# A hybrid mLSTM block: mLSTM of x in two chunks with a second state, and two scalings of the output by ScalarE

## The chip, the cores and the metric

The kernel runs on one core of a Trainium2 chip. The core has five engines that run side by side, each taking its own instructions in order: TensorE (PE in the profile; its weight loads are PEld), VectorE (DVE), ScalarE (ACT), GpSimd (POOL) and SyncE (SP), which here issues most DMAs. The metric is the device time of one execution in microseconds; lower is better. Three executions of the kernel before took 1530.03 to 1533.87 us, median 1532.19 us.

## The reference

Two layers work on x (512 tokens of 1024) and a context (256 tokens). Each layer has a token mixer (an mLSTM of 4 heads of 128, a Fourier mix and a convolution), whose outputs are joined and projected, and an MLP of width 4096. The last layer needs no output of the context. In the mLSTM a matrix state is carried over the tokens, forward and backward; the context is passed through first, and x starts from the context's last state. The reference does it in chunks of 64:

```python
def step(carry, inp):
    C, n, m = carry
    ...
    m_t = jnp.maximum(a, jnp.max(D, axis=-1))
    w_inter = jnp.exp(a - m_t)
    S = jnp.einsum('bhld,bhsd->bhls', qc, kc) * jnp.exp(D - m_t[..., None])
    num = w_inter[..., None] * jnp.einsum('bhed,bhld->bhle', C, qc) + jnp.einsum('bhls,bhse->bhle', S, vc)
    den = w_inter * jnp.einsum('bhd,bhld->bhl', n, qc) + jnp.sum(S, axis=-1)
    h = num / jnp.maximum(jnp.abs(den), jnp.exp(-m_t))[..., None]
    ...
    C_new = decay[..., None, None] * C + jnp.einsum('bhs,bhse,bhsd->bhed', ws, vc, kc)
    n_new = decay[..., None] * n + jnp.einsum('bhs,bhsd->bhd', ws, kc)
```

Forward and backward results are added, and each head's row of 128 is normalized: mean subtracted, multiplied by one over the deviation.

## The kernel before

Tokens stand as 6 blocks of 128: blocks 0 and 1 are the context, 2 to 5 are x. Matrix products with weights are done in three matmuls of a short and a rest part: a weight chunk comes by DMA into a tile `raw`, ScalarE rounds it to `hi` (line 219) and VectorE takes the rest as `lo` (line 220), for two weights ahead of their use. There are 3 tiles `raw`, 6 `hi` and 5 `lo`.

The mixer goes through the chunks of the input projection, for each head q, k and o (`stationary`, line 463). When a head's o is done, its `mlstm` is put on a list, and one of its three parts is written behind the matmuls of each of the next chunks: so the heads run between the projections of the next head. The three parts are these.

- First part: q and k are split into two parts each (`split`, lines 230 and 233). Scores are `scores` (line 793), three matmuls. For the context (layer 0 only) two key blocks against 256 queries; for x, four key blocks against all 512 queries. ScalarE makes the exponential weights from the stabilizers (line 836), GpSimd masks the block on the diagonal (line 771), VectorE multiplies by the scores (line 838). The context's state is made from k, transposed (line 818) and weighted by ScalarE (line 822), times v (line 842), copied to the tile `cs` (line 844). `qs` is q weighted for the state.
- Second part: for each block and direction TensorE sums the state term `qs` times `cs` and one term for each key block that the direction sees (line 862). All these are fp32 and 129 columns wide; column 128 is the denominator. Then `head_out`: VectorE makes the denominators, scales the forward part by the one (line 752), adds the backward part scaled by the other (line 753), and takes the moments. When all blocks of a group are there, GpSimd takes the power for the deviation (line 767), and VectorE subtracts the mean and scales (line 867).
- Third part: TensorE transposes the group's blocks (line 777), and ScalarE and VectorE apply gain and gate.

PSUM has 4 banks `mm` for projections and 4 `aux` for everything else. The order of the instructions on each engine is made by a scheduler, which places each when it expects its inputs to be ready, by a priority that follows the order in which the program is written. SyncE issues the loads; the stabilizers at a sequence's end are loaded to `m0` (line 647).

Of the kernel before, what the change touches and what calls it, by code (L numbers as in the profile page):

```python
# [50 lines left out]
XQ = CTX + 1  # L51
PAD = 15
# [12 lines left out]
def build(tc, a):  # L65
# [408 lines left out]
    def layer(l, res, nbg, first=None):  # L474
# [169 lines left out]

        m0 = small.tile([128, 2, 4], F32, tag="m0", name=nm("m0"))
        for d, t0 in ((0, CTX - 1), (1, 0)):
            dma(m0[:, d, :], md[l][4 * d:4 * d + 4, t0].partition_broadcast(128))

        def gate_columns():
            for q in range(2):  # L650
                ps = aux()
                for i in range(3):
                    T.transpose(ps[:, 128 * i:128 * i + 128], pm[:, 128 * (3 * q + i):128 * (3 * q + i) + 128], ident)
                v4 = ps[:, :384].rearrange("p (b g d n) -> p b g d n", b=3, g=2, d=2)
                for i in range(3):
                    V.tensor_copy(pcol[:, 3 * q + i], v4[:, i, 0, :, 0:4])
                    S.activation(em[:, 3 * q + i], v4[:, i, 1, :, 0:4], AF.Exp, scale=-1.0)
            for j in range(CB):
                V.tensor_tensor(wc[:, j], pcol[:, j], m0, ALU.subtract)
            S.activation(wc, wc, AF.Exp)  # L660

# [80 lines left out]
        def kcol(j):  # L742
            return 128 * j if j < CB else XQ + 128 * (j - CB)

        def head_out(ps, b, h, hn, ba):
            den = ps[:, 128:258:129]
            d = ty(2, "d")
            V.tensor_tensor(d, den, em[:, b, :, h], ALU.max)
            V.scalar_tensor_tensor(d, den, -1.0, d, ALU.mult, ALU.max)
            rd = ty(2, "rd")  # L750
            V.reciprocal(rd, d)
            V.tensor_scalar(hn, ps[:, 0:128], rd[:, 0:1], None, ALU.mult)
            V.scalar_tensor_tensor(hn, ps[:, 129:257], rd[:, 1:2], hn, ALU.mult, ALU.add)
            moments(hn, ba)
# [28 lines left out]
        def mlstm(h, q, k, to):  # L783
# [10 lines left out]

            if not last:
                mb = c2().rearrange("p (d t) -> p d t", d=2)
                dma(mb, mdv[h, :, 0:CTX].partition_broadcast(128))
                qk = aux()
                E = t4().rearrange("p (j d t) -> p j d t", j=2, d=2)
                for j in range(2):  # L800
                    scores(qk[:, 256 * j:256 * j + 256], 128 * j, 0, CTX)
                for j, d in ((0, 0), (0, 1), (1, 0), (1, 1)):
                    lo, hi = (128 * j, CTX) if d == 0 else (0, 128 * j + 128)
                    S.activation(E[:, j, d, lo:hi], mb[:, d, lo:hi], AF.Exp, scale=-1.0,
                                 bias=pcol[:, j, d, h:h + 1])
                    masked(E[:, j, d, 128 * j:128 * j + 128], d == 0)
                    V.tensor_tensor(E[:, j, d, lo:hi], E[:, j, d, lo:hi], qk[:, 256 * j + lo:256 * j + hi], ALU.mult)

                def c_terms(b, d, E=E):
                    js = range(0, b + 1) if d == 0 else range(b, CB)  # L810
                    return [(E[:, j, d, 128 * b:128 * b + 128], vt[h][:, j, :]) for j in js]
                groups.append((0, range(CB), c_terms))
            mb = t4().rearrange("p (d t) -> p d t", d=2)
            dma(mb, mdv[h, :, CTX:TOK].partition_broadcast(128))

            kp = aux()
            for j in range(CB):
                T.transpose(kp[:, 128 * j:128 * j + 128], k[:, 128 * j:128 * j + 128], ident)
            kw = c2().rearrange("p (d j n) -> p d j n", d=2, j=CB)
            for d in range(2):  # L820
                for j in range(CB):
                    S.activation(kw[:, d, j, :], kp[:, 128 * j:128 * j + 128], AF.Copy, scale=wc[:, j, d, h:h + 1])
            qs = t4().rearrange("p (d t) -> p d t", d=2)
            for d in range(2):
                S.activation(qs[:, d, :], mb[:, d, :], AF.Exp, scale=-1.0, bias=m0[:, d, h:h + 1])
            V.tensor_tensor(qs, qs, q[:, XQ:XQ + SEQ].unsqueeze(1).to_broadcast([128, 2, SEQ]), ALU.mult)
            Es = {}
            for j in range(CB, NB):
                qk = aux()
                scores(qk, kcol(j), XQ, SEQ)  # L830
                E = t4().rearrange("p (d t) -> p d t", d=2)
                Es[j] = E
                s0 = 128 * (j - CB)
                for d in range(2):
                    lo, hi = (s0, SEQ) if d == 0 else (0, s0 + 128)
                    S.activation(E[:, d, lo:hi], mb[:, d, lo:hi], AF.Exp, scale=-1.0, bias=pcol[:, j, d, h:h + 1])
                    masked(E[:, d, s0:s0 + 128], d == 0)
                    V.tensor_tensor(E[:, d, lo:hi], E[:, d, lo:hi], qk[:, lo:hi], ALU.mult)
# [15 lines left out]
            for t0, bs, terms in groups:  # L854
# [600 lines left out]
```

## Time and profile before

| | |
|---|---|
| median of 3 runs | 1532.19 us |
| the profiled execution | 1534.91 us, span 1532.9 us |
| TensorE busy | 1488.5 us, 97% |
| VectorE busy | 1101.4 us, 72% |
| ScalarE busy | 754.9 us, 49% |
| GpSimd busy | 94.0 us, 6% |
| granted TensorE clock | 0.998 |

The profile is of one execution; a time in it is counted from the start of the span. A group's row gives line, engine, operation, what it writes and reads, the shapes, how often (x), the busy time in us, the mean duration of one in ns, and the idle time of the engine before it with what ended it. Matmuls overlap, so a row's mean duration is more than what one takes from its neighbours. Lines are those of the kernel before unless the text speaks of the changed one.

### The profile page before, as it was taken

To read this page: it belongs to the slowest core of one execution; us is meant where nothing else is said; L and a number is where in the kernel's file an instruction comes from. 1 tells how busy PE (TensorE), PEld (TensorE's weight loads), DVE (VectorE), ACT (ScalarE), POOL (GpSimd) and SP (SyncE) were. 2 spreads that over 40 slices of the span, in tenths; PEclk is the share of its full clock that TensorE was granted. 3 is DMA by queue.
4 is the path that set the end of the run, shared out by engine and by line. 5 is a ranking of instruction groups with operands and counts; after the bars stand their busy time and mean duration, and the time that the engine had idled before them with its cause. 6 is when DMAs were issued, how large, how long until landed. Compare 5 with 4: busy or idle time off the path is not lost. (4 is left out here: it accounts for less than half of the span.)

```text
span 1532.9 us, 23301 instructions
## 1 busy us (share of the span) xinstructions
PE 1488.5 (97%) x8926; PEld 1303.6 (85%) x8926; DVE 1101.4 (72%) x2129; ACT 754.9 (49%) x1471; POOL 94.0 (6%) x233
## 2 busy tenths in 40 slices
PE   7999999999999999999999999999999999999998
PEld 4878888887888898898988979877888889999887
DVE  3359997754899886666865575898756886677666
ACT  4634245535745352442534576544437665555544
POOL 0002012200100000000000010111101000000000
PEclk9999999999999999999999999999999999999999
DMA  8445435523532452442622343422224133332224
GB/s 330 140 159 186 158 125 194 199 83 117 186 124 92 146 189 76 158 132 88 193 86 80 99 171 105 129 78 78 88 71 166 66 111 110 111 109 91 83 94 148
DMA packets 66015, 197.30 MB, mean 129 GB/s; under 512 B 11952, under 2 KB 14416, under 8 KB 65904
## 3 DMA queue, kind: packets, MB, share of 16 engines
q1 hardware_dynamic: 64464, 191.10, 37.5%
q0 software_dynamic: 1440, 4.72, 1.0%
q8 instruction: 70, 1.15, 0.3%
q14 instruction: 41, 0.34, 0.1%
HBM read 183.13 MB, written 12.66 MB: 128 GB/s over the span
## 5 line engine op out<-in xcount | busy, mean ns | idle before, releaser
L219 ACT ACTIVATE hi<-raw 128x1024 fp32r<-128x1024 f32 (+1 forms) x245 | 244.1, 999 | 397.0 <-PE mm L1052 134.9
L1052 PE MATMUL mm<-hi,t 128*128 128x512 f32 (+1 forms) x1296 | 406.1, 391 | 0.0
L220 DVE TENSOR_TENSOR lo<-raw,hi 128x1024 fp32r<-128x1024 f32 (+1 forms) x245 | 280.7, 1148 | 75.4 <-ACT hi L219 37.6
L1052 PEld LDWEIGHTS mm<-hi,t 128*128 128x128 f32 x1296 | 242.4, 188 | 54.7 <-DVE t L1220 0.4
L1052 PE MATMUL mm<-lo,t 128*128 128x512 f32 (+1 forms) x648 | 253.7, 391 | 0.0
L463 PE MATMUL mm<-hhi,hi 128*128 128x256 f32 (+1 forms) x576 | 168.3, 336 | 0.0
L463 PE MATMUL mm<-hlo,hi 128*128 128x256 f32 (+1 forms) x576 | 166.0, 332 | 0.0
L463 PE MATMUL mm<-hhi,lo 128*128 128x256 f32 (+1 forms) x576 | 165.0, 331 | 0.0
L1052 PEld LDWEIGHTS mm<-lo,t 128*128 128x128 f32 x648 | 121.8, 188 | 26.0
L1121 PE MATMUL mm<-hhi,hi 128*128 128x384 f32 (+1 forms) x448 | 139.5, 311 | 3.0 <-ACT c L1147 1.8
L1121 PE MATMUL mm<-hhi,lo 128*128 128x384 f32 (+1 forms) x448 | 138.5, 309 | 1.5 <-DVE lo L220 1.5
L1220 DVE TENSOR_TENSOR t<-mm,t 128x512 f32<-128x512 f32 x120 | 81.8, 688 | 79.5 <-PE mm L1052 79.4
L1121 PE MATMUL mm<-hlo,hi 128*128 128x384 f32 (+1 forms) x448 | 138.4, 309 | 0.0
L463 PEld LDWEIGHTS mm<-hhi,hi 128*128 128x128 f32 x576 | 107.1, 188 | 15.0 <-issue 2.5
L463 PEld LDWEIGHTS mm<-hhi,lo 128*128 128x128 f32 x576 | 108.3, 188 | 11.0
L463 PEld LDWEIGHTS mm<-hlo,hi 128*128 128x128 f32 x576 | 108.0, 188 | 11.0 <-issue 0.4
L679 DVE SCALAR_TENSOR_TENSOR t<-t,half,t 128x783 f32<-128x783 f32 (+1 forms) x120 | 102.3, 889 | 0.4
L1121 PE MATMUL mm<-t,hi 128*128 128x384 f32 (+1 forms) x448 | 97.4, 308 | 0.0
L1121 PEld LDWEIGHTS mm<-hhi,hi 128*128 128x128 f32 x448 | 84.4, 188 | 6.8 <-ACT c L1147 3.0
L1121 PEld LDWEIGHTS mm<-hhi,lo 128*128 128x128 f32 x448 | 84.3, 188 | 1.9 <-DVE lo L220 1.9
L1121 PEld LDWEIGHTS mm<-hlo,hi 128*128 128x128 f32 x448 | 84.4, 188 | 1.2
L233 DVE TENSOR_TENSOR t<-c,t 128x256 fp32r<-128x256 f32 (+1 forms) x132 | 62.2, 478 | 31.9 <-ACT t L230 31.5
(245 smaller groups left out, 2732.2 us busy)
## 6 DMA issues: line engine op xcount, KB each, us to landing
raw<-w SPq DMA_DIRECT2D x128, 512.0 KB, 4.3
raw<-w_at SPq DMA_DIRECT2D x48, 512.0 KB, 3.6
raw<-w_a SPq DMA_DIRECT2D x44, 512.0 KB, 4.3
raw<-w_c SPq DMA_DIRECT2D x32, 512.0 KB, 3.5
xd<-t SPq DMA_DIRECT2D x20, 512.0 KB, 2.9
raw<-w_o SPq DMA_DIRECT2D x16, 512.0 KB, 6.0
t<-xd SPq DMA_DIRECT2D x20, 256.0 KB, 6.0
t<-x SPq DMA_DIRECT2D x8, 512.0 KB, 6.0
```

The costliest lines, as they stand in the source:

```text
L219: S.activation(hi[:, r0:n0], raw[:, r0:n0], AF.Copy)
L220: V.tensor_tensor(lo[:, r0:n0], raw[:, r0:n0], hi[:, r0:n0].bitcast(F32), ALU.subtract)
L233: V.tensor_tensor(blk_lo, src, blk_hi.bitcast(F32), ALU.subtract)
L463: T.matmul(o[:, :n], wp[:, k, :], hp[:, k, t0:t0 + n], start=k == 0 and i == 0, stop=k == KB - 1 and i == 2)
L679: V.scalar_tensor_tensor(o, u[j][:, o0 + k:o1 + k], w, o, ALU.mult, ALU.add)
L1052: T.matmul(ps, hp[:, 128 * b:128 * b + 128], wp[:, f % 2, c0:c1], start=f == fs[0] and at[0] == 0 and n == 0, stop=f == fs[-1] and at[1] = ...
L1121: T.matmul(ps[:, :HN], wp[:, K2 * j + k, :], hp, start=first and k == 0 and i == 0, stop=k == K2 - 1 and i == 2, skip_group_check=True)
L1220: V.tensor_tensor(ac_, ps, ac_, ALU.add)
```

## The change

The 512 tokens of x are taken as two chunks of 256 (blocks 2, 3 and 4, 5). Scores are made within a chunk alone. What one chunk gives to the other comes through a state: forward the first chunk starts from the context's state `cs` and the second from a new state `cs1`, backward it is the other way round. `cs1` is the context's state times a decay, plus the weighted k of the chunk in between times v; for it four blocks of k are transposed and weighted as well, and two more columns of stabilizers are loaded to `m1`. The function `weighted` now serves the context and both chunks. Beside this, both scalings of a block's output are done by ScalarE; the second needs minus the mean times the scale, which VectorE makes in one small instruction a group.

```diff
+        m1 = small.tile([128, 2, 4], F32, tag="m1", name=nm("m1"))
+        dec = small.tile([128, 2, 4], F32, tag="dec", name=nm("dec"))
+        wx = small.tile([128, 4, 4], F32, tag="wx", name=nm("wx"))
+        for d, t0, t1 in ((0, CTX - 1, CTX + CH - 1), (1, 0, CTX + CH)):
             dma(m0[:, d, :], md[l][4 * d:4 * d + 4, t0].partition_broadcast(128))
+            dma(m1[:, d, :], md[l][4 * d:4 * d + 4, t1].partition_broadcast(128))
...
+            for i in range(4):
+                V.tensor_tensor(wx[:, i], pcol[:, CB + i, i // 2], m1[:, i // 2], ALU.subtract)
+            S.activation(wx, wx, AF.Exp)
+            V.tensor_tensor(dec, m0, m1, ALU.subtract)
+            S.activation(dec, dec, AF.Exp)
...
-            V.tensor_scalar(hn, ps[:, 0:128], rd[:, 0:1], None, ALU.mult)
+            S.activation(hn, ps[:, 0:128], AF.Copy, scale=rd[:, 0:1])
             V.scalar_tensor_tensor(hn, ps[:, 129:257], rd[:, 1:2], hn, ALU.mult, ALU.add)
...
+            def weighted(mb, kc, q0, blk):
+                qk = aux()
+                E = t4().rearrange("p (j d t) -> p j d t", j=2, d=2)
+                for j in range(2):
+                    scores(qk[:, CH * j:CH * j + CH], kc + 128 * j, q0, CH)
...
+            kp = aux()
+            for i in range(4):
+                T.transpose(kp[:, 128 * i:128 * i + 128], k[:, XQ + 128 * i:XQ + 128 * i + 128], ident)
+            for i in range(4):
+                S.activation(kx[:, i, :], kp[:, 128 * i:128 * i + 128], AF.Copy, scale=wx[:, i, h:h + 1])
...
-            for j in range(CB, NB):
-                qk = aux()
-                scores(qk, kcol(j), XQ, SEQ)
...
+            Ex = [weighted(mb[:, :, CH * c:CH * c + CH], XQ + CH * c, XQ + CH * c, CB + 2 * c) for c in range(2)]
...
+            cp = aux()
+            for d in range(2):
+                for j in range(2):
+                    i = 2 * d + j
+                    T.matmul(cp[:, 129 * d:129 * d + 129], kx[:, i, :], vt[h][:, CB + i, :], start=j == 0, stop=j == 1)
+            cs1 = c2()[:, :258]
+            for d in range(2):
+                dd = slice(129 * d, 129 * d + 129)
+                V.scalar_tensor_tensor(cs1[:, dd], cs[:, dd], dec[:, d, h:h + 1], cp[:, dd], ALU.mult, ALU.add)
...
-                js = range(CB, b + 1) if d == 0 else range(b, NB)
-                return [(qs[:, d, s0:s0 + 128], cs[:, 129 * d:129 * d + 129])] + \
-                       [(Es[j][:, d, s0:s0 + 128], vt[h][:, j, :]) for j in js]
+                c = (b - CB) // 2
+                return [(qs[:, d, s0:s0 + 128], (cs if c == d else cs1)[:, 129 * d:129 * d + 129])] + \
+                    within(Ex[c], b, CB + 2 * c, d)
...
+                nb_ = ty(4, "nb")[:, :len(bs)]
+                V.scalar_tensor_tensor(nb_, ba[:, 0:len(bs), 0], -1.0, r, ALU.mult, ALU.mult)
                 for i in range(len(bs)):
                     hb = hn[:, 128 * i:128 * i + 128]
-                    V.tensor_scalar(hb, hb, ba[:, i, 0:1], r[:, i:i + 1], ALU.subtract, ALU.mult)
+                    S.activation(hb, hb, AF.Identity, scale=r[:, i:i + 1], bias=nb_[:, i:i + 1])
```

The scheduler orders the instructions anew, inside the heads alone. In the changed kernel lines stand lower: scores are line 801, the transposes of k 835 (context) and 841 (x), the states 855 and 862, the output 884, the scalings 760 and 891, the rounding of weights 220.

TensorE before, the end of the scores of the third head of layer 0 (`aux` are PSUM banks, `t` short and rest parts of k and q):

```order
L793 MATMUL aux_2733<-t_421_2667,t_423_2669 128x512
L793 MATMUL aux_2733<-t_422_2668,t_423_2669 128x512
L793 MATMUL aux_2733<-t_421_2667,t_424_2670 128x512
L793 MATMUL aux_2744<-t_421_2667,t_423_2669 128x512
L793 MATMUL aux_2744<-t_422_2668,t_423_2669 128x512
L793 MATMUL aux_2744<-t_421_2667,t_424_2670 128x512
```

TensorE now, at the same place, with both states behind the scores:

```order
L801 MATMUL aux_2776<-t_426_2701,t_428_2703 128x256
L801 MATMUL aux_2776<-t_427_2702,t_428_2703 128x256
L801 MATMUL aux_2776<-t_426_2701,t_429_2704 128x256
L855 MATMUL aux_2796<-t_59_240,t_434_2733 128x129 x4
L862 MATMUL aux_2803<-t_59_240,t_434_2733 128x129 x4
```

A key block's three matmuls are half as wide, and the second state has come up directly behind the first; before, the first state followed 23 matmuls of the projection later.

TensorE before, the output of x's first block in the same head (`c` is the state, the rest are weights times values):

```order
L862 MATMUL aux_2917<-c_441_2760,t_431_2707 128x129
L862 MATMUL aux_2917<-t_59_240,t_433_2715 128x129
L862 MATMUL aux_2917<-c_441_2760,t_431_2707 128x129
L862 MATMUL aux_2917<-t_59_240,t_433_2715 128x129
L862 MATMUL aux_2917<-t_59_240,t_435_2726 128x129
L862 MATMUL aux_2917<-t_59_240,t_437_2737 128x129
L862 MATMUL aux_2917<-t_59_240,t_439_2748 128x129
```

TensorE now, the same block:

```order
L884 MATMUL aux_2968<-c_443_2801,t_437_2750 128x129
L884 MATMUL aux_2968<-t_59_240,t_439_2757 128x129
L884 MATMUL aux_2968<-c_445_2808,t_437_2750 128x129
L884 MATMUL aux_2968<-t_59_240,t_439_2757 128x129 x2
```

Seven matmuls a block have become five, and the backward direction reads the second state.

ScalarE before, in the second head of layer 0, while that head's output is made (line 219 rounds weights, 779 and 963 are a gain and a gate):

```order
L735 ACTIVATE t_387_2455<-mm_2281,dk_234 128x256
L735 ACTIVATE t_387_2455<-mm_2282,dk_234 128x512
L219 ACTIVATE hi_2485<-raw_2487 128x1024
L219 ACTIVATE hi_2596<-raw_2598 128x1024
L779 ACTIVATE t_322_2144<-aux_2541,half_236 128x256
```

ScalarE now, in the same place:

```order
L746 ACTIVATE t_392_2489<-mm_2320,dk_234 128x512
L760 ACTIVATE c_357_2369<-aux_2371,rd_2378 128x128
L760 ACTIVATE c_357_2369<-aux_2385,rd_2392 128x128
L760 ACTIVATE c_370_2407<-aux_2409,rd_2418 128x128
L220 ACTIVATE hi_2519<-raw_2521 128x1024
L891 ACTIVATE c_357_2369<-c_357_2369,nb_2403,lr_2401 128x128 x2
L760 ACTIVATE c_370_2407<-aux_2425,rd_2434 128x128
L760 ACTIVATE c_370_2407<-aux_2441,rd_2450 128x128
L760 ACTIVATE c_370_2407<-aux_2457,rd_2466 128x128
L891 ACTIVATE c_370_2407<-c_370_2407,nb_2477,lr_2475 128x128 x4
L220 ACTIVATE hi_2630<-raw_2632 128x1024
L787 ACTIVATE t_326_2167<-aux_2575,half_236 128x256
```

Both scalings of the two groups stand around a rounding of weights: three of x's four first scalings come behind it.

## Rows read from the trace of the kernel before

**Rows 1.** The page: the span, TensorE's busy time, its granted clock.

```profile
span 1532.9 us, 23301 instructions
PE 1488.5 (97%) x8926; PEld 1303.6 (85%) x8926; DVE 1101.4 (72%) x2129; ACT 754.9 (49%) x1471; POOL 94.0 (6%) x233
PEclk9999999999999999999999999999999999999999
```

**Rows 2.** Busy time by stretch: the heads of layer 0 and of layer 1.

```profile
core 0: us, PE busy (x) PEld busy (x) DVE busy (x) ACT busy (x) POOL busy (x), PEclk, DMA share, GB/s
150.00:330.00 180.00, 176.74 (x1225) 152.77 (x1224) 152.16 (x395) 78.82 (x162) 30.31 (x68) 1.00 0.49 163
980.00:1140.00 160.00, 154.03 (x906) 132.73 (x905) 134.84 (x314) 71.50 (x142) 24.68 (x66) 1.00 0.28 89
```

**Rows 3.** TensorE's groups by shape: scores of x, output, context's state.

```profile
L862 PE MATMUL aux<-t,t 128*128 128x129 f32 x368 | 52.2, 274 | 0.0
...
L793 PE MATMUL aux<-t,t 128*128 128x512 f32 x96 | 26.3, 408 | 1.6 <-DVE t L233 1.6
L862 PE MATMUL aux<-c,t 128*128 128x129 f32 x128 | 25.2, 278 | 0.6 <-DVE d L748 0.4 <-DVE c L704 0.2
...
L842 PE MATMUL aux<-t,c 128*128 128x129 f32 x64 | 8.6, 277 | 1.3 <-DVE t L838 1.3
```

**Rows 4.** TensorE's timeline in the second head (start, us, engine, line, names, count).

```profile
206.07 0.87 PE L793 MATMUL aux<-t,t 128*128 128x256 f32 x6
206.78 0.38 PE L818 MATMUL aux<-ident_sb,t 128*128 128x128 f32 x2
...
209.01 2.31 PE L793 MATMUL aux<-t,t 128*128 128x512 f32 x9
211.16 0.39 PE L463 MATMUL mm<-hhi,hi 128*128 128x512 f32 x1
211.38 1.05 PE L842 MATMUL aux<-t,c 128*128 128x129 f32 x8
212.28 0.51 PE L273 MATMUL aux<-sel_sb,c 128*128 128x8 f32 x4
```

**Rows 5.** TensorE's timeline: eight transposes and what follows.

```profile
264.18 1.04 PE L696 MATMUL aux<-ident_sb,t 128*128 128x128 f32 x8
265.06 1.50 PE L862 MATMUL aux<-t,t 128*128 128x129 f32 x12
```

**Rows 6.** Waits of TensorE in the whole run: us, times, longest.

```profile
PE aux L777 <- DVE c L867: 4.9, 4, 1.7
...
PE aux L793 <- DVE t L233: 1.6, 2, 0.8
...
PE aux L862 <- DVE d L748: 0.4, 1, 0.4
```

**Rows 7.** Groups by shape: both scalings on VectorE, a scaled copy on ScalarE.

```profile
L752 DVE TENSOR_SCALAR c<-aux,rd 128x128 f32<-128x128 f32 x40 | 13.4, 335 | 0.0
...
L867 DVE TENSOR_SCALAR c<-c,ba,lr 128x128 f32<-128x128 f32 x40 | 11.4, 349 | 10.2 <-POOL lr L767 10.2
...
L822 ACT ACTIVATE c<-aux,wc 128x128 f32<-128x128 f32 x32 | 9.4, 382 | 0.0
```

**Rows 8.** Timelines: ScalarE's two longest waits beside outputs, and a wait of TensorE.

```profile
227.87 1.06 ACT L219 ACTIVATE hi<-raw 128x1024 fp32r<-128x1024 f32 x1 [5.38 <-DMA raw<-w_c]
...
281.24 1.06 ACT L219 ACTIVATE hi<-raw 128x1024 fp32r<-128x1024 f32 x1 [16.68 <-PE mm L463]
...
286.95 1.12 DVE L867 TENSOR_SCALAR c<-c,ba,lr 128x128 f32<-128x128 f32 x4 [0.93 <-POOL lr L767]
...
287.45 0.30 PE L777 MATMUL aux<-ident_sb,c 128*128 128x128 f32 x1 [1.69 <-DVE c L867]
```

**Rows 9.** The tile of the stabilizer columns: its loads, and their landing.

```profile
L647 SPq DMA_DIRECT2D m<-md x4: 371/426/493, 95.5 to 979.5; - x4
...
DMA to landing us min/median/max: 5.5/5.5/5.5
```

More of the change, by code (lines that the diff above doesn't have):

```diff
@@ L51 @@
 XQ = CTX + 1
+CH = 256
 PAD = 15
@@ L645, in layer @@
         m0 = small.tile([128, 2, 4], F32, tag="m0", name=nm("m0"))
-        for d, t0 in ((0, CTX - 1), (1, 0)):
+        m1 = small.tile([128, 2, 4], F32, tag="m1", name=nm("m1"))
+        dec = small.tile([128, 2, 4], F32, tag="dec", name=nm("dec"))
+        wx = small.tile([128, 4, 4], F32, tag="wx", name=nm("wx"))
+        for d, t0, t1 in ((0, CTX - 1, CTX + CH - 1), (1, 0, CTX + CH)):
             dma(m0[:, d, :], md[l][4 * d:4 * d + 4, t0].partition_broadcast(128))
+            dma(m1[:, d, :], md[l][4 * d:4 * d + 4, t1].partition_broadcast(128))
         def gate_columns():
@@ L740, in short_conv @@
             return q
-        def kcol(j):
-            return 128 * j if j < CB else XQ + 128 * (j - CB)
         def head_out(ps, b, h, hn, ba):
@@ L793, in scores, with within @@
                     T.matmul(out, kp_[:, kc:kc + 128], qp[:, q0:q0 + n], start=i == 0, stop=i == 2)
+            def weighted(mb, kc, q0, blk):
[3 more added lines that the diff above has]
+                    scores(qk[:, CH * j:CH * j + CH], kc + 128 * j, q0, CH)
+                for j, d in ((0, 0), (0, 1), (1, 0), (1, 1)):
+                    lo, hi = (128 * j, CH) if d == 0 else (0, 128 * j + 128)
+                    S.activation(E[:, j, d, lo:hi], mb[:, d, lo:hi], AF.Exp, scale=-1.0,
+                                 bias=pcol[:, blk + j, d, h:h + 1])
+                    masked(E[:, j, d, 128 * j:128 * j + 128], d == 0)
+                    V.tensor_tensor(E[:, j, d, lo:hi], E[:, j, d, lo:hi], qk[:, CH * j + lo:CH * j + hi], ALU.mult)
+                return E
+            def within(E, b, blk, d):
+                i = b - blk
+                js = range(0, i + 1) if d == 0 else range(i, 2)
+                return [(E[:, j, d, 128 * i:128 * i + 128], vt[h][:, blk + j, :]) for j in js]
             if not last:
@@ L797, in mlstm @@
                 dma(mb, mdv[h, :, 0:CTX].partition_broadcast(128))
-                qk = aux()
[L799 to L812, printed above, removed]
+                Ec = weighted(mb, 0, 0, 0)
+                groups.append((0, range(CB), lambda b, d: within(Ec, b, 0, d)))
             mb = t4().rearrange("p (d t) -> p d t", d=2)
             dma(mb, mdv[h, :, CTX:TOK].partition_broadcast(128))
+            kt = t4()
+            kw = kt[:, 0:512].rearrange("p (d j n) -> p d j n", d=2, j=CB)
+            kx = kt[:, 512:1024].rearrange("p (i n) -> p i n", i=4)
             kp = aux()
@@ L818, in mlstm @@
                 T.transpose(kp[:, 128 * j:128 * j + 128], k[:, 128 * j:128 * j + 128], ident)
-            kw = c2().rearrange("p (d j n) -> p d j n", d=2, j=CB)
             for d in range(2):
@@ L822, in mlstm @@
                     S.activation(kw[:, d, j, :], kp[:, 128 * j:128 * j + 128], AF.Copy, scale=wc[:, j, d, h:h + 1])
+            kp = aux()
[3 more added lines that the diff above has]
+                S.activation(kx[:, i, :], kp[:, 128 * i:128 * i + 128], AF.Copy, scale=wx[:, i, h:h + 1])
             qs = t4().rearrange("p (d t) -> p d t", d=2)
             for d in range(2):
-                S.activation(qs[:, d, :], mb[:, d, :], AF.Exp, scale=-1.0, bias=m0[:, d, h:h + 1])
+                for c in range(2):
+                    m_ = m0 if c == d else m1
+                    S.activation(qs[:, d, CH * c:CH * c + CH], mb[:, d, CH * c:CH * c + CH], AF.Exp, scale=-1.0,
+                                 bias=m_[:, d, h:h + 1])
             V.tensor_tensor(qs, qs, q[:, XQ:XQ + SEQ].unsqueeze(1).to_broadcast([128, 2, SEQ]), ALU.mult)
-            Es = {}
-            for j in range(CB, NB):
-                qk = aux()
-                scores(qk, kcol(j), XQ, SEQ)
[L831 to L838, printed above, removed]
+            Ex = [weighted(mb[:, :, CH * c:CH * c + CH], XQ + CH * c, XQ + CH * c, CB + 2 * c) for c in range(2)]
             cp = aux()
```

## The prediction

> **What bounds the kernel now.** I read the page first, then the busy time by stretch, then the groups of TensorE by shape, then the timeline of TensorE inside one head, and last who waited for whom. The reader is to see on the page that TensorE is busy for 97% of the span at the full granted clock [rows 1]. The stretches say whether that also holds where the change is: in 150 to 330 us (heads of layer 0) TensorE is busy for 176.74 of 180 us, in 980 to 1140 us (heads of layer 1) for 154.03 of 160 us, granted clock 1.00 in both [rows 2]. VectorE stands at 152 of 180 and 135 of 160 us, ScalarE under half. So TensorE's own work sets the time of these stretches; at most 3.3 + 6.0 = 9.2 us of idle time can be won there, and every matmul taken out shortens the span unless something makes TensorE wait.
>
> **What one matmul costs on the path.** The duration in a group's row overstates it, since matmuls overlap: what counts is the distance between starts. In the timeline of one head [rows 4] nine score matmuls of 512 columns start at 209.01 and the next instruction at 211.16, so (211.16 - 209.01) / 9 = 0.239 us each. Six of 256 columns go from 206.07 to 206.78, 0.118 us each. The fp32 matmuls of 129 columns (states, and state or weights times values) stand in the trace as two records each: the code has 32 of them on line 842 and 248 on line 862, the trace 64 and 368 + 128 [rows 3]. Eight such records go from 211.38 to 212.28, 0.1125 us each, so 0.225 us a matmul. Eight transposes of 128 x 128 go from 264.18 to 265.06, 0.110 us each [rows 5].
>
> **The change on TensorE.** There are 4 heads in each of 2 layers, 8 in all.
> Scores of x: before, 4 key blocks against all 512 queries, 3 matmuls each: 12 of 512 columns a head, 96 in all [rows 3]. After, 2 chunks of 2 key blocks against 256 queries: 12 of 256 columns. 96 x (0.239 - 0.118) = 11.6 us gone.
> Output of x: before, a block of 128 tokens sums in both directions together 2 state terms and 5 weight terms, 7; after, 2 and 3, so 5. 4 blocks x 2 terms x 8 heads = 64 matmuls x 0.225 = 14.4 us gone.
> Second state: 4 matmuls a head more, 32 x 0.225 = 7.2 us; and 4 transposes of k a head more, 32 x 0.110 = 3.5 us.
> The context's part of layer 0 is as before. Sum: -11.6 - 14.4 + 7.2 + 3.5 = -15.3 us of TensorE.
> The row of the transposes says 0.110 us between starts, though one lasts longer than that. [...]
>
> **The change on the other engines.** VectorE loses the two scalings, 40 blocks each, 13.4 + 11.4 = 24.8 us [rows 7], and 1024 of 2560 columns a head of weights times scores; it gains two short sums for the second state and a handful of columns for gates. ScalarE gains 80 scalings and 32 weighted copies of k; the nearest row is the scaled copy from PSUM of the same 128 x 128, 9.4 us for 32, so 0.294 us each [rows 7]: 112 x 0.294 = 33 us spread over 340 us in which it is busy for 150 [rows 2]. Lower bound 0 (hidden), upper bound 33 us if all of it stood on the path; I take 0 for the work itself, since ScalarE idles for more than half of both stretches, and charge the waits below. The two more loads of stabilizer columns per layer go with two that take 5.5 us to land [rows 9], and nothing reads them before the heads start; they stand in front of two or three weight loads in SyncE's queue, about 0.4 us each, and TensorE waits for no weight in these stretches; with that cover gone it would be 2 x 2 x 0.4 = 1.6 us.
>
> **What gets later.** A head's output is a chain: VectorE's denominators, scaling one, sum of both directions, moments, GpSimd's power, scaling two, then TensorE's transposes. That chain already ends late in four places, 4.9 us in all [rows 6]. Two steps of it move to ScalarE: three more hand-overs between engines and one more small VectorE instruction. A hand-over can be read where TensorE waited: the first scaling starts at 286.95 and takes 0.35 us [rows 7, 8], the transpose starts at 287.45, so 0.15 us. Three hand-overs and a small instruction of about the same are 0.6 us for a group. 12 groups (8 of x, 4 of the context): between -4.9 us (VectorE, relieved of 25 us, makes the old waits vanish) and +7.2 us (each group is exposed). I take +3: the four places exposed already cost 2.4, and one more.
>
> **The forecast.** -15.3 + 3 = -12.3 us. The profiled execution took 1534.91 us, 2.0 more than its span of 1532.9 [rows 1]; the sum is against that and makes it 1522.6. The median of the runs before is 1532.19, and from it I get 1519.9, say 1520.0. If the added waits come out at 0 it is 1517, at 7.2 it is 1524, and some 2 us either way for the order that the scheduler makes anew inside the heads: 1514 to 1526 as this case's own range.
>
> **Rivals.**
> ScalarE's order holds the scalings back (slower). ScalarE takes its instructions in order, and between the scalings stand roundings of weights (line 219) that wait for a load or for a buffer that TensorE gives back: 5.38 us until 227.87 in the second head of layer 0, and 16.68 us until 281.24 in the third [rows 8]. In the new order three of the four scalings of x stand behind such a rounding in the second head, one in the third. Against it: in the second head TensorE has 46 matmuls of the next chunk, half of them of 256 and half of 512 columns, 46 x (0.118 + 0.239) / 2 = 8 us, before it needs those results, and in layer 1 all four scalings of a head stand ahead of the next rounding. If the cover did not hold, VectorE would stand too, since the sum of both directions waits behind, and with it the lo parts of the weights. It decides from 15.3 / 8 = 1.9 us of TensorE's waiting a head on. If TensorE stood for both waits of the rows above, 22 us: 1532.2 - 15.3 + 22 = 1539, slower.
> [...]
> Part of the gain is lost (between). Scores at half the width leave TensorE 1.4 us a head sooner, so the weights (exponentials, masks, products) have 1.4 us less time before the output needs them. Against it: a head has 1536 such columns to make where it had 2560, and today the output waits 0.4 us in all at line 862 [rows 6]. Exposed in 6 of 8 heads it is 8 us: 1525 to 1528.
> Narrow scores are no cheaper (same). If a score matmul were paced by its weight load and not by its columns, 11.6 us of the sum would be missing and the rest, -3.7 + 3, is nothing: 1531.5. Against it: the six of 256 columns at 0.118 us [rows 4].
> The relief counts (faster still). VectorE is the busiest engine after TensorE in the stretches; if the 24.8 us taken from it remove the waits of rows 6 (4.9 + 1.6 + 0.4 = 6.9 us): 1532.2 - 15.3 - 6.9 = 1510.
>
> **How the numbers follow.** Forecast 0.66, relief 0.11, part lost 0.11, ScalarE's order 0.07, narrow scores 0.05. Range for 8 in 10: from 1512, which leaves out the far half of the relief, to 1529, which leaves out ScalarE's order and narrow scores. What a measurement of this kernel can tell from no change is about 0.3%, 4.6 us, so faster means under 1527.6. Faster: forecast 0.66 + relief 0.11 + three quarters of part lost 0.08 = 0.85. Slower: most of ScalarE's order, 0.06. The same: the rest, 0.09.
>
> **What would show it.** In the changed profile line 801's group (scores) should hold 120 matmuls of 256 columns at 0.118 us between starts, and none of 512; the fp32 matmuls of 129 columns of states and output should be 368 + 128 = 496 records against 560; TensorE's busy time should fall by about 15 us and both stretches of the heads should be some 6 to 8 us shorter, with the MLP stretches as long as before. VectorE should fall by 25 us or more, ScalarE rise by about 30. Waits of TensorE for line 891 should stand near 5 to 8 us in all. The forecast is wrong if waits for line 760 or for the weights of the output sum to over 10 us, if the rounding of weights (line 220) makes TensorE wait, or if the MLP stretches change.

## The result, and the profile after

The kernel after took 1516.5 us (median of 4 runs, 1514.5 to 1519.7) against 1532.7 for the kernel before, timed beside it: a ratio of 0.9899, 95% interval 0.9875 to 0.9922, so 12 to 19 us faster. Run once more beside other kernels it took 1513.1 us (1511.9 to 1515.9), ratio 0.9873 [0.9860, 0.9887], 17 to 21 us faster. Forecast were 1520.0 us, 1512 to 1529.

The page after, the lines of [rows 1]:

```profile
span 1516.2 us, 23325 instructions
PE 1471.9 (97%) x8894; PEld 1291.9 (85%) x8894; DVE 1078.8 (71%) x2087; ACT 786.1 (52%) x1603; POOL 86.8 (6%) x233
```

TensorE is busy 16.6 us less than in [rows 1] and the span is 16.7 us shorter; the idle time, 44 us, is the same. VectorE lost 22.6 us, ScalarE gained 31.2. TensorE is still the bound, at 97%. This is the profile of the first run; in that of the second run the span is 1510.0 us and TensorE is busy for 1469.0. What sets the two apart is told among the experiments.

Where the time went is read from the timeline: the first matmul of each stage (start in us, duration, engine, line, names, count). Before:

```profile
78.47 0.60 PE L463 MATMUL mm<-hhi,hi 128*128 128x256 f32 x2
...
435.28 0.39 PE L1052 MATMUL mm<-hi,t 128*128 128x512 f32 x1
...
917.23 0.28 PE L510 MATMUL mm<-hi,hhi 128*128 128x264 f32 x1
...
959.50 0.48 PE L463 MATMUL mm<-hhi,hi 128*128 128x512 f32 x1
...
1206.21 0.40 PE L1052 MATMUL mm<-hi,t 128*128 128x512 f32 x1
```

After:

```profile
79.15 0.59 PE L464 MATMUL mm<-hhi,hi 128*128 128x256 f32 x2
...
428.41 0.40 PE L1076 MATMUL mm<-hi,t 128*128 128x512 f32 x1
...
908.78 0.28 PE L511 MATMUL mm<-hi,hhi 128*128 128x264 f32 x1
...
950.59 0.48 PE L464 MATMUL mm<-hhi,hi 128*128 128x512 f32 x1
...
1190.94 0.39 PE L1076 MATMUL mm<-hi,t 128*128 128x512 f32 x1
```

The rows are the start of layer 0's mixer (projections, heads, output projection), of its MLP, of layer 1's values, of its mixer, of its MLP. Layer 0's mixer went from 356.8 to 349.3 us, layer 1's from 246.7 to 240.4: 13.9 us together. The other stages, whose program did not change, are 2.8 us shorter: 481.9 to 480.4 for the first MLP, 1.5 of it. In the 14 profiles of this study, which share these stages, they summed to 925 to 931 us, so 2.8 us there is scatter.

The stretches that answer to [rows 2], with their columns, moved to where the heads now lie:

```profile
150.00:322.00 172.00, 169.47 (x1213) 148.57 (x1212) 139.26 (x360) 101.57 (x243) 32.41 (x76) 1.00 0.51 174
970.00:1130.00 160.00, 154.99 (x915) 133.93 (x914) 126.92 (x301) 85.46 (x201) 22.75 (x62) 0.99 0.27 90
```

TensorE is as full as before (98.5% and 96.9%); VectorE fell to 81% and 79% of them, ScalarE rose to 59% and 53%.

In the heads, TensorE's groups by shape after (line, engine, operation, names, shapes, count | busy us, mean ns | idle before), to set against [rows 3]:

```profile
L884 PE MATMUL aux<-t,t 128*128 128x129 f32 x240 | 38.1, 274 | 0.0
...
L884 PE MATMUL aux<-c,t 128*128 128x129 f32 x128 | 24.9, 276 | 0.0
...
L801 PE MATMUL aux<-t,t 128*128 128x256 f32 x120 | 18.4, 294 | 2.0 <-DVE t L814 1.1 <-DVE t L234 0.9
...
L855 PE MATMUL aux<-t,t 128*128 128x129 f32 x64 | 8.7, 276 | 0.0
L862 PE MATMUL aux<-t,t 128*128 128x129 f32 x64 | 8.6, 276 | 0.0
...
L841 PE MATMUL aux<-ident_sb,t 128*128 128x128 f32 x32 | 4.8, 272 | 0.0
```

No score matmul of 512 columns is left, and the records of 129 columns are 240 + 128 + 64 + 64 = 496. Their pace stands in the timeline of the second head, where [rows 4] stood:

```profile
208.41 1.67 PE L801 MATMUL aux<-t,t 128*128 128x256 f32 x12
209.92 1.05 PE L855 MATMUL aux<-t,t 128*128 128x129 f32 x8
```

Twelve scores take 209.92 - 208.41 = 1.51 us, 0.126 us each (median of all 120 starts 0.121). TensorE's waits after, against [rows 6]:

```profile
PE aux L785 <- ACT c L891: 4.2, 4, 1.9
...
PE aux L801 <- DVE t L814: 1.1, 1, 1.1
```

The wait for a group's last scaling was 4.9 us for VectorE's L867 and is 4.2 us for ScalarE's L891. No wait of TensorE names line 760.

### The profile page after: what moved, and what is told of

The parts are those of the page before. It is cut to its first block, busy times and chain, and to the rows that moved or that the text cites. A ratio compares the mean times of both kernels' runs of the same rounds, so it can differ in the third digit from the quotient of the medians.

```text
span 1516.2 us, 23325 instructions
## 1 busy us (share of the span) xinstructions
PE 1471.9 (97%) x8894; PEld 1291.9 (85%) x8894; DVE 1078.8 (71%) x2087; ACT 786.1 (52%) x1603; POOL 86.8 (6%) x233
## 5 line engine op out<-in xcount | busy, mean ns | idle before, releaser
L464 PEld LDWEIGHTS mm<-hlo,hi 128*128 128x128 f32 x576 | 108.6, 190 | 11.3 <-issue 1.0
```

The source lines that it names most:

```text
L464: T.matmul(o[:, :n], wp[:, k, :], hp[:, k, t0:t0 + n], start=k == 0 and i == 0, stop=k == KB - 1 and i == 2)
```

## The experiments

Each was timed in five rounds beside the kernel before, which took 1533 to 1534 us in all of them. Times in us. "Mixers" is the sum of both layers' mixers in the one execution that was profiled, read as above (before 603.5, after 589.6).

| kernel | median | ratio to before, 95% | mixers |
|---|---|---|---|
| after, again | 1513.1 | 0.9873 [0.9860, 0.9887] | 585.0 |
| chunks only | 1514.1 | 0.9876 [0.9860, 0.9893] | 584.9 |
| first scaling on ScalarE | 1514.7 | 0.9883 [0.9869, 0.9896] | 584.4 |
| second scaling on ScalarE | 1514.3 | 0.9882 [0.9865, 0.9900] | 590.0 |
| scalings only | 1541.1 | 1.0050 [1.0034, 1.0067] | 609.5 |
| scalings only, again | 1541.4 | 1.0051 [1.0036, 1.0065] | 610.8 |
| scalings only, early md | 1541.7 | 1.0052 [1.0039, 1.0065] | 614.2 |
| scores twice | 1529.0 | 0.9971 [0.9961, 0.9981] | 598.4 |
| zero terms | 1533.5 | 1.0001 [0.9988, 1.0013] | 603.8 |
| one state | 1510.9 | 0.9852 [0.9840, 0.9865] | 578.2 |
| blocks of 128 | 1519.7 | 0.9917 [0.9904, 0.9931] | 589.0 |
| wide state | 1516.7 | 0.9894 [0.9874, 0.9914] | 587.7 |

**The two parts of the change apart.** The chunks alone are the kernel after with both scalings back on VectorE:

```diff
-            S.activation(hn, ps[:, 0:128], AF.Copy, scale=rd[:, 0:1])
+            V.tensor_scalar(hn, ps[:, 0:128], rd[:, 0:1], None, ALU.mult)
...
-                    S.activation(hb, hb, AF.Identity, scale=r[:, i:i + 1], bias=nb_[:, i:i + 1])
+                    V.tensor_scalar(hb, hb, ba[:, i, 0:1], r[:, i:i + 1], ALU.subtract, ALU.mult)
```

> The kernel after with both scalings of a head's output back on VectorE, so the two chunks and the second state alone. Theory: the gain is TensorE's shorter program, and the scalings change the end by -5 to +7 us (taken +3 in the prediction, 0 by the waits of the trace after); so this stands 3 us below to 3 us above the kernel after, 1514 to 1520 us, and VectorE is busy about 25 us longer than after, ScalarE about 33 us less, with TensorE waiting for VectorE's L889 in place of ScalarE's L891, about 4 us. Rival: VectorE's relief carries part of the gain; then this is 4 us or more above the kernel after, 1521 us or more.

The scalings alone are the kernel before with the two lines changed the other way:

> The kernel before with both scalings of a head's output on ScalarE and nothing else. Theory: within 0 to +5 us of the kernel before, 1532 to 1537 us, as the chain of output is a few tenths of a us longer a group and TensorE's program is the same. Rival (VectorE's relief carries part of the gain): 4 us or more below the kernel before, 1528 us or less. Rival of the prediction (ScalarE's order holds scalings back): 1539 us or more.

The chunks alone carry the whole gain: 1514.1 us, 16 to 21 below before. The scalings alone make the kernel before slower by 7.6 us [5.2 to 10.3], more than the theory's 0 to 5 and past the 1539 us of the second rival. The first runs left it open whether they cost the kernel after 2.4 us, so it was run again, with each scaling by itself:

> The kernel after once more, unchanged, beside the three below, so that a few us can be told. Theory: 1515 to 1519 us, 0.990 of the kernel before, and TensorE's waits for the group's last scaling (L785 or the line 464 beside it, on ScalarE's L891) between 4 and 10 us in sum. Rival (the 2.4 us between the first medians of the kernel after and of the chunks alone were scatter): 1514 us or less, level with the chunks alone.

> The kernel after with only the scaling by the reciprocal (L760) on ScalarE; that by the moments is back on VectorE. Theory, after the trace (the last scaling is what TensorE meets): the 2 to 3 us that both scalings cost lie in the other one, so this is level with the chunks alone, 1513 to 1516 us. Rival (each block's scaling waits in ScalarE's queue for VectorE's reciprocal, L760 behind L759, and holds back what stands behind it): 2 to 3 us above the chunks alone, 1516 us or more.

> The kernel after with only the scaling by the moments (L891) on ScalarE; that by the reciprocal is back on VectorE. Theory: this one carries the 2 to 3 us, as a small VectorE instruction and two hand-overs stand between GpSimd's power and it, so it is level with the kernel after, 1516 to 1519 us. Rival: level with the chunks alone, 1513 to 1515 us.

The rivals hold in the first and the third; the second theory named the right time, but there was no cost to be found in either half. After again, the chunks alone and both halves lie between 1513.1 and 1514.7 us, nearer to each other than the intervals are wide; the first run of the kernel after (1516.5) stands 1.8 us above them, and its interval touches theirs. TensorE's waits say the same. This is the row of the chunks alone:

```profile
PE aux L785 <- DVE c L889: 4.4, 5, 1.7
```

It is 4.2 with both scalings on ScalarE. Which engine scales makes no difference in the kernel after that these runs can tell.

**Two profiles of one program.** The two profiled executions of the kernel after differ by 4.6 us in the mixers. These are the mixers of both layers before, after, and after again, with the columns of [rows 2] (TensorE's busy time comes first, its granted clock third from the end):

```profile
78.47:435.28 356.81, 348.92 (x2303) 297.46 (x2302) 269.27 (x599) 163.03 (x338) 47.42 (x108) 1.00 0.47 158
959.50:1206.21 246.71, 239.05 (x1379) 204.96 (x1377) 190.80 (x396) 126.71 (x248) 29.63 (x74) 1.00 0.32 103
...
79.15:428.41 349.26, 342.50 (x2287) 293.66 (x2285) 256.69 (x570) 181.48 (x412) 41.96 (x108) 1.00 0.47 161
950.59:1190.94 240.35, 233.79 (x1362) 201.24 (x1361) 181.16 (x381) 140.12 (x306) 27.69 (x70) 0.99 0.32 106
...
78.12:424.30 346.18, 340.69 (x2288) 292.75 (x2287) 256.44 (x570) 181.26 (x412) 41.99 (x108) 1.00 0.48 162
946.08:1184.92 238.84, 232.22 (x1363) 200.15 (x1361) 181.03 (x381) 140.14 (x306) 28.15 (x70) 1.00 0.32 107
```

With the same program TensorE is busy for 576.3 us of the mixers in the first profile and for 572.9 in the second, and idle for 13.3 and 12.1. The 3.4 us of busy time belong to two stretches of the first profile in which the granted clock is 0.50, against 1.00 in the rest of its mixers:

```profile
104.58:107.99 3.41, 3.41 (x16) 2.33 (x14) 1.17 (x2) 1.06 (x1) 0.00 (x0) 0.50 0.78 293
1026.18:1029.59 3.41, 3.41 (x11) 2.55 (x12) 3.15 (x5) 1.67 (x5) 0.00 (x0) 0.50 0.46 143
```

Each stands right behind a wait of TensorE of 1.88 us, the one for a load of weights, the other for ScalarE's L891. The second profile has the same two waits, 1.55 and 1.95 us long, and behind them the clock stays at 1.00. The timelines behind the first of these waits, in the first profile and in the second:

```profile
104.46 1.02 PE L248 MATMUL aux<-raw,csil 128*32 128x256 f32 x8 [1.88 <-DMA raw<-w_a]
...
106.86 0.84 PE L464 MATMUL mm<-hhi,hi 128*128 128x256 f32 x2
107.50 0.74 PE L464 MATMUL mm<-hlo,hi 128*128 128x256 f32 x2
```

```profile
103.12 0.64 PE L248 MATMUL aux<-raw,csil 128*32 128x256 f32 x8 [1.55 <-DMA raw<-w_a]
...
104.84 0.51 PE L464 MATMUL mm<-hlo,hi 128*128 128x256 f32 x2
105.20 0.51 PE L464 MATMUL mm<-hhi,lo 128*128 128x256 f32 x2
```

A pair of projection matmuls starts 0.64 us before the next pair in the one (107.50 - 106.86) and 0.36 us in the other (105.20 - 104.84). So 3.4 of the 4.6 us are not the program's, since it is the same in both. The mixers of the kernel before, of after again, of the chunks alone and of the first scaling alone hold no stretch at 0.50, and between these the mixers gained 18.5 to 19.1 us (585.0, 584.9 and 584.4 against 603.5). Those of the second scaling alone hold 10.2 us of it: its profiled execution took 1520.3 us, 6 above its median.

**TensorE's prices on the path.** Scores twice puts back 96 matmuls of 256 columns; zero terms adds one more term to each output sum of the observations, with a tile of zeros as weights:

```diff
+                    for _ in range(2 if blk >= CB else 1):
+                        scores(qk[:, CH * j:CH * j + CH], kc + 128 * j, q0, CH)
```

```diff
-                    within(Ex[c], b, CB + 2 * c, d)
+                    within(Ex[c], b, CB + 2 * c, d) + [(zed, vt[h][:, b, :])]
```

> The kernel after with every score product of the observations made twice into the same place (96 more matmuls of 256 columns at 0.118 us from start to start, 11.3 us of TensorE). Theory (score columns are on the path at their own pace): about 11 us above the kernel after, 1525 to 1530 us. Rival (the scores are made while TensorE would wait for the weights anyway, so their columns are nearly free): less than 6 us above, 1522 us or less.

> The kernel after with one more term of zeros in every output sum of the observations (64 more fp32 matmuls of two records of 0.1125 us, 14.4 us of TensorE: what the chunks took out there). Theory: about 14 us above the kernel after, 1528 to 1533 us. Rival (the terms are hidden beside the waits for the weights or beside the chain of output): less than 7 us above, 1523 us or less.

Both were paid in full and more: 12.5 to 15.9 us above the two runs of the kernel after for 11.3 us of scores, 17.0 to 20.4 us for 14.4 us of terms (1533.5 is half a us past the theory's range); in the mixers 8.8 to 13.4 and 14.1 to 18.7. Both rivals (under 6 and under 7 us) fall. Not all that came on top is the price of the terms: in the profile of zero terms TensorE waits 3.6 us at the scores (L803 for VectorE's L816), and the granted clock is 0.50 from 259.86 to 263.27, behind that wait.

The second state's price was asked by leaving it out (k's four transposes, kx, the four state matmuls and cs1):

```diff
-                return [(qs[:, d, s0:s0 + 128], (cs if c == d else cs1)[:, 129 * d:129 * d + 129])] + \
+                return [(qs[:, d, s0:s0 + 128], cs[:, 129 * d:129 * d + 129])] + \
```

> The kernel after without the second state: both chunks take the context's state, and the transposes of k, the scaled k and the four state matmuls of a head are left out (that part of the computation is left out). Theory: what the second state costs on TensorE comes back, 8 x (4 x 0.110 + 4 x 0.225) = 10.7 us, 1502 to 1508 us. Rival (the second state lies beside waits of TensorE and costs nothing): 1512 us or more.

The time fell by 2.2 to 5.6 us of the 10.7, between theory and rival. The mixers of the profiled run fell by 6.8 to 11.4 us, and the stages that this edit leaves alone were 5 to 6 us longer than in the kernel after, so the total says little. A part was given back inside the mixers, in one wait of TensorE for the context's weights times scores:

```profile
PE aux L850 <- DVE t L814: 2.9, 1, 2.9
```

This wait is not the edit's own. It ends a chain that begins with a late load (`c<-md`), and it comes and goes: the kernel after has it with 1.1 us at L801 in its first profile and not in its second, the second scaling alone with 2.8 us, zero terms with the 3.6 us named above. What the second state costs on the path stays open.

**Why the scalings cost in the kernel before.** A second run decides whether the 7.6 us are real:

> The kernel before with both scalings on ScalarE, once more. In the kernel after they cost nothing that the runs can tell (1513.1 and 1516.5 us with them, 1514.1 without), in the kernel before 7.6 us [5.2 to 10.3]. Theory (a cost of the old score order: ScalarE is late with the weights, VectorE frees the score buffer late, TensorE waits at L793): 1538 to 1544 us again, with waits of 2 us or more at L793. Rival (a scatter between placements of one program on the chip): 1531 to 1536 us.

They are: 1541.4, and the whole of it is in layer 0's mixer (364.8 us against 356.8; layer 1's 246.1 against 246.7). Of these 8.0 us TensorE is idle for 4.6 (12.5 against 7.9) and busy for 3.3 with the same matmuls (352.2 against 348.9). The longest new wait is a chain through five engines, in the timelines of this run:

```profile
251.10 0.39 SPq L797 DMA_DIRECT2D c<-md  x1
...
259.67 1.49 ACT L804 ACTIVATE t<-c,pcol 128x256 f32<-128x256 f32 x4 [4.52 <-DMA c<-md]
...
260.25 1.27 POOL L771 TENSOR_SCALAR_AFFINE_SELECT t<-t 128x128 f32<-128x128 f32 x4 [8.22 <-ACT t L804]
...
260.58 1.40 DVE L807 TENSOR_TENSOR t<-t,aux 128x256 f32<-128x256 f32 x4 [5.06 <-POOL t L771]
...
262.03 2.93 PE L793 MATMUL aux<-t,t 128*128 128x512 f32 x6 [4.09 <-DVE t L807]
```

Read from below: TensorE stands 4.09 us for VectorE, which has yet to multiply what is in a score buffer, VectorE stands 5.06 us for the mask, GpSimd with the mask 8.22 us for the exponential, and ScalarE with that 4.52 us for a load issued at 251.10 and landed 8.6 us later, behind three weight loads. In the kernel before the same load was issued at 249.05, and the exponential began at 253.89 without a wait. During the wait the granted clock fell to 0.50, and TensorE ran on at this clock:

```profile
260.49:267.31 6.82, 5.28 (x14) 4.31 (x15) 5.40 (x10) 6.82 (x18) 3.36 (x13) 0.50 0.05 22
```

The six score matmuls took 2.93 us here and 1.58 in the kernel before. The first run of the scalings has the same wait, 3.0 us, and the granted clock is 0.50 from 258.63 to 262.03. So the load was issued earlier:

```diff
             elif n == "q":
                 got["q"] = short_conv(outs, lambda k: cols[:, C_QK + 8 * k + j:C_QK + 8 * k + j + 1], ranges)
+                if not last:
+                    got["mb"] = c2().rearrange("p (d t) -> p d t", d=2)
+                    dma(got["mb"], mdv[j, :, 0:CTX].partition_broadcast(128))
...
-                mb = c2().rearrange("p (d t) -> p d t", d=2)
-                dma(mb, mdv[h, :, 0:CTX].partition_broadcast(128))
+                mb = got["mb"]
```

> The kernel before with both scalings on ScalarE (which twice came out 7.5 us above the kernel before), and with the load of md for a head's context part (c<-md, L797) put behind the head's projection of q: the third of these loads then stands ahead of two loads of w_f and three of w_o in SyncE's order, and not behind them. Theory: 4 of the 7.5 us are one wait, where TensorE (L793) waits for VectorE (L807), that for GpSimd's mask, that for ScalarE's exponential (L804) and that for c<-md, which lands 7 to 8.6 us after its issue behind the w_o loads; with the load early the wait at L793 is under 1 us and the time 1534 to 1538 us. Rival (the scalings' own place in ScalarE's order costs the 7.5 us, and the load is late only because all is): 1539 to 1543 us, the wait at L793 still 2 us or more.

That wait went, the time did not: 1541.7, in the rival's range. In its place stand several, one of 2.1 us at L793 too (rows of the waits in 78 to 430 us):

```profile
PE aux L777 <- ACT c L868: 2.2, 1, 2.2
PE aux L793 <- ACT t L230: 2.1, 1, 2.1
...
PE aux L793 <- DVE t L233: 1.5, 1, 1.5
```

Layer 0's mixer took 368.1 us, 14.0 of them with TensorE idle, and behind the first two of these waits the granted clock is 0.50 again (198.34 to 201.75 and 300.74 to 304.15). So, as far as these three profiles show, the 7.6 us are waits of TensorE and the clock of 0.50 with them, and the late load was where the delay showed, or one delay among several. The edit also moved other loads in SyncE's order, so it isn't a clean removal. Why the scalings bring such waits in the old score order, and only in layer 0, stays open.

**Two tries for a better kernel.** Blocks of 128 carries the idea on: four chunks, a state at every inner border, both scalings on VectorE. Its core:

```diff
-            Ex = [weighted(mb[:, :, CH * c:CH * c + CH], XQ + CH * c, XQ + CH * c, CB + 2 * c) for c in range(2)]
+            for i in range(4):
+                scores(qk[:, 128 * i:128 * i + 128], XQ + 128 * i, XQ + 128 * i, 128)
...
+                return [(qs[:, d, 128 * i:128 * i + 128], state(i, d)), (E[:, i, d, :], vt[h][:, b, :])]
```

> The chunks alone (both scalings on VectorE), but with four chunks of 128 in place of two of 256: a state at each of the three inner borders in either direction, scores of a block with itself only. On TensorE a head has 12 score matmuls of 128 columns in place of 12 of 256, 16 output matmuls in place of 20 (4 x 0.225 us less) and 6 state matmuls in place of 4 (2 x 0.225 us more): 0.45 us less a head with score matmuls that cost as much at 128 columns as at 256, 1.15 us less if they cost half. Theory (TensorE's work on its path is what counts): 3.6 to 9.2 us below the chunks alone over 8 heads, 1505 to 1511 us. Rival (the chain of three states and the smaller instructions of ScalarE and VectorE become late): level with the chunks alone or above, 1514 us or more.

It came out 5.6 us above the chunks alone, so the theory falls and the rival holds. Its TensorE work is smaller by little more than the low end of what was expected, since narrower scores were hardly cheaper. The timeline of the second head:

```profile
204.73 1.45 PE L804 MATMUL aux<-t,t 128*128 128x128 f32 x12
206.02 1.11 PE L868 MATMUL aux<-t,c 128*128 128x129 f32 x8
```

(206.02 - 204.73) / 12 = 0.108 us for 128 columns, where 256 columns had 0.126 in the kernel after. By medians of starts (scores 0.112 and 0.121, and 32 fp32 records fewer at 0.112) the mixers hold 4.4 us less work than the chunks alone, and yet they took 4.0 us longer. TensorE is idle for 3.5 us more (15.1 against 11.6), in part on the longer chain: it waits for the copy of the context's state and for the sums of states, and in layer 1 longer for the last scaling (2.9 us, with the chunks alone 1.9). Waits of layer 1's mixer:

```profile
PE aux L788 <- DVE c L911: 2.9, 1, 2.9
PE aux L906 <- ACT c L870: 1.0, 1, 1.0
```

Behind the wait of 2.9 us the granted clock is 0.50 from 1030.94 to 1034.34. The rest is spread thinly over the mixers, and another 2.6 us lie in stages that the edit doesn't touch. How much of the 5.6 us is the blocks' own stays open.

Wide state asks what paces a narrow matmul:

```diff
-                for j in range(CB):
-                    T.matmul(cp[:, 129 * d:129 * d + 129], kw[:, d, j, :], vt[h][:, j, :], start=j == 0, stop=j == CB - 1)
+            for j in range(CB):
+                T.matmul(cp[:, 0:258], kc_[:, 128 * j:128 * j + 128], kt[:, 258 * j:258 * j + 258],
+                         start=j == 0, stop=j == CB - 1)
```

> The kernel after with the context's state made from unscaled k blocks and v blocks scaled once for each direction, so two matmuls of 258 fp32 columns a head stand in place of four of 129 (the same sums, scaled on the other factor; ScalarE has one copy more a head). After the blocks of 128, where a score matmul of 128 columns began 0.112 us after the one before (0.121 at 256), theory A: a matmul below some 256 columns takes 0.11 us however few they are, so the records of 258 columns take about 0.12 us, 3.4 us go from TensorE over 8 heads, and the time is 1509 to 1514 us. Theory B: fp32 records go by their columns, 0.22 us at 258, and nothing is won: 1513 to 1517 us. The start-to-start times in the trace decide, the whole only if it moves by 3 us or more.

The trace decides for theory B, and the time (1516.7) agrees. The timeline:

```profile
207.76 1.03 PE L856 MATMUL aux<-t 128*128 128x258 f32 x4
208.72 0.63 PE L248 MATMUL aux<-raw,csil 128*32 128x256 f32 x6
```

(208.72 - 207.76) / 4 = 0.24 us a record of 258 columns (median 0.217), twice the 0.112 of 129. No kernel of this study that computes the whole beats the kernel after by more than its interval.

## Why the prediction was right, and where its numbers were off

**TensorE's work sets the time of the heads.** Right. -15.3 us were forecast; by the medians of all starts the matmuls that changed hold 14.7 us less. The chunks alone carry the whole gain, and work put back was paid for in full. The mixers lost 7.5 and 6.3 us in the first profile, inside the 6 to 8 forecast for the heads' stretches, and 10.6 and 7.9 in the second, where the clock stayed at 1.00.

**Distance between starts as the price.** Right for the outputs and transposes: 496 records at 0.112 us, transposes at 0.109. For the scores it was a little low: 0.121 us, not 0.118, by the median of all 120. Counted by the duration of one (272 ns, L841) the 32 transposes would have been 8.7 us and the sum -10; the starts are 0.109 us apart, and the change gained more than 10 us.

**The chain of output, taken at +3 us.** This is the term that was mis-sized. Its working said that two steps on ScalarE add three hand-overs and a small instruction, 0.6 us a group, and charged five groups. Measured: the exposed wait went from 4.9 to 4.2 us, where 5 to 8 were forecast, and with and without the scalings the kernel is the same within 2.4 us. All of TensorE's idle time in the mixers fell, from 15.6 us to 13.3 in the first profile, 12.1 in the second and 11.6 with the chunks alone. So the waits stand at some -2 to -4 us in the sum, not at +3. Why they fell is not shown: the chunks alone have it too, so it is not the scalings that left VectorE. VectorE hardly waits for the first scaling, as its sum of both directions shows (groups by shape):

```profile
L891 ACT ACTIVATE c<-c,nb,lr 128x128 f32<-128x128 f32 x40 | 16.7, 483 | 16.4 <-DVE nb L888 16.4
...
L760 ACT ACTIVATE c<-aux,rd 128x128 f32<-128x128 f32 x40 | 14.1, 364 | 30.8 <-DVE d L756 12.8 <-DVE rd L759 9.8 <-issue 4.8
L761 DVE SCALAR_TENSOR_TENSOR c<-aux,rd,c 128x128 f32<-128x128 f32 x40 | 13.2, 345 | 1.8 <-ACT c L760 1.5
```

ScalarE stands 30.8 us before the first scaling, mostly for VectorE's denominators and reciprocal; VectorE stands 1.5 us for ScalarE. The estimate of ScalarE's time, 0.294 us a scaling, was low (0.353 and 0.418: busy time over 40), and it cost nothing, as forecast. (VectorE fell by 22.6 us where 25 or more were forecast, since the small instruction and the second state take some back; ScalarE rose by 31.2, about the 30 forecast.) With this term at 0 the sum is -15.3 us, 1516.9 from the median of 1532.19. That the first measurement lies within 0.5 us of it is luck: in its profiled execution stretches at a clock of 0.50 took back about what the waits gave. With the measured -14.7 and -3.5 the sum is -18.2 us; the mixers lost 18.5 in the second profile, and four of the five runs with the chunks came out 18.4 to 20.1 us below the kernel before.

**ScalarE's order holds scalings back (a rival).** It did not decide here: no wait of TensorE names line 760. But in the old score order the same two lines cost 7.5 us, twice. That the time is close to the 1539 us that the rival named does not show its mechanism, since no wait in layer 0's mixer was for a rounding of weights. The prediction treated the two parts of the change as terms of a sum. They interact: -19.4 for the chunks, +7.6 for the scalings, and both together -16.2 and -20.1 us, not -11.8.

**Narrow scores are no cheaper (a rival).** Wrong at 256 columns, where the change works (0.121 us against 0.236 before), right at 128, where the blocks tried it (0.112 us against 0.121). That 128 columns take hardly less than 256 was not in the prediction and was not needed for it. Whether the weight load sets this pace is not shown: the record of one load lasts 189 ns (L801's, in the kernel after), longer than the distance between starts, and no run here changed the load alone.

**Loads of stabilizer columns.** The step said that nothing reads them before the heads start. That was wrong: the difference m0 - m1 (line 670) was put early in the order, and VectorE stood 4.35 us there for the load, ScalarE 10.07 us for VectorE. VectorE's and ScalarE's timelines:

```profile
103.24 0.17 DVE L670 TENSOR_TENSOR dec<-m,m 128x8 f32<-128x8 f32 x1 [4.35 <-DMA m<-md]
...
103.44 0.21 ACT L671 ACTIVATE dec<-dec 128x8 f32<-128x8 f32 x1 [10.07 <-DVE dec L670]
```

It cost nothing that TensorE's waits show. In the kernel before ScalarE stood in the same place for 12.87 us for a weight load.

**Part of the gain lost (a rival).** It did not come. One wait of 1.1 us, for weights times scores (L814), points that way in the first profile, for the context's and behind a late load; the second has none.

**The relief counts (a rival).** Its reason fell, since the chunks alone, with both scalings back on VectorE, gain as much. Its size came in part: TensorE's idle time fell by 2.3 to 4.0 us, where the rival had 6.9.

## What to carry to other kernels

On an engine that is busy for 97% of the span, count a change by the distance between starts of the instructions that it removes, from the timeline and not from durations. Here that number was right within 1 us for TensorE's own work (-15.3 forecast, -14.7 by the starts). The time moved by 1 to 6 us more, when work was removed and when it was put back, through waits and through the clock behind them; and where the second state was left out, by 5 to 9 us less than it. Work moved between two engines off the bound cost nothing here that the runs can tell (the scalings are 14.1 + 16.7 us of ScalarE; 1513.1 and 1516.5 us with both on it, 1514.1 without), but in the old score order the same move cost 7.6 us: measure such a move in the kernel that will have it, not beside another version. Splitting further did not pay: from 256 to 128 columns a score went only from 0.121 to 0.112 us between starts, TensorE was idle for 3.5 us more, and the blocks came out 5.6 us above the chunks alone. Before two profiles are compared at a few us, look at the granted clock of their stretches: two at 0.50 were 3.4 us here.

## What the runs showed of the hardware that was not expected

A score matmul of 512, 256 and 128 columns starts 0.236, 0.121 and 0.112 us after the one before (medians of starts of all such groups): the first halving took off 0.115 us, the second 0.009. A plain fp32 record of 129 and 258 columns takes 0.112 and 0.217 us, so there the columns still count at a width where the scores' matmuls no longer get cheaper by fewer of them.

During waits of 1.88 to 4.1 us, or soon behind them, TensorE's granted clock fell to 0.50 in some executions and stayed at 1.00 in others, once with the same program and nearly the same waits (1.88 and 1.88 us, 1.55 and 1.95 us). The two stretches cost 3.4 us of the mixers. The medians of that program in two sessions differ by as much (1516.5 and 1513.1); the four executions of the first had mean granted clocks of 0.995 to 0.998, those of the second 0.996 to 0.999. Stages whose program is the same in all kernels differ by 6 us in their sum. So a difference of 0.2% between two kernels can't be told here.
